# A Fox attention head's division cut into halves of 512 columns between the row maxima, with one row maximum a turn sooner

## The chip, the cores and the metric

The kernel runs on one core of one Trainium2 chip. The metric is the device time of one execution in microseconds; the time of a kernel is the median of its runs.

## What is computed

The reference is one decoder block over 1024 tokens of width 1024. Two branches read one normalised input: a state-space recurrence and an attention with forget gates (Fox). Gates merge them, one projection follows, then attention over 256 memory tokens and a feed-forward layer. The change lies in the Fox attention, 8 heads of 64 columns. Its core in the reference, cut:

```python
s = jnp.einsum('bhqd,bhkd->bhqk', qb, kh).astype(jnp.float32) * scale
s = s + cb[..., :, None] - cum[..., None, :]
s = jnp.where(causal, s, -jnp.inf)
p = jax.nn.softmax(s, axis=-1)
return jnp.einsum('bhqk,bhkd->bhqd', p.astype(vh.dtype), vh)
```

## The kernel before

Every product is made of three matmuls: an operand is split into a high part (a copy on ScalarE) and a low part (the rest, a subtraction on VectorE), and high times high, high times low and low times high are added in one bank (mm3, L173 to L175; split, L183 and L184). PSUM has eight banks: three named mm for projections and row maxima, two named sc for scores, two named pv for values, one named misc.

The Fox attention is one loop over heads (Fox.run), which takes 355 to 571 us of the span. Each head has twelve units (qc, kt): query half qc of 512 columns against key block kt of 128, causal, so units at the diagonal have 512, 384, 256 or 128 columns. A unit is:

- two score matmuls into a sc bank (L1793, L1794), at the diagonal a mask addition on VectorE (L1796), and the exponential on ScalarE (L1800) into pf;
- the split of pf: high part ph on ScalarE (L1805) and low part pl on VectorE (L1806); for the units (0,2), (1,0), (1,2) and (1,4) ph is a cast on VectorE (L1802) and pl a subtraction on GpSimd (L1803);
- one or two units later the products with the values: L1818 and L1819 with ph, L1825 with pl, into a pv bank. At the end of a query half ScalarE copies the bank to num (L1827).

The values carry a column of ones, so row 64 of num is the softmax's denominator. After a head's last unit finish(h) sends it through three small DMAs on SyncE's queue (rc L1836, rd_d L1838, rb L1840) with a reciprocal between them, so that rb holds the reciprocals on 64 partitions. The division divide(h-1) comes in the next head's units: VectorE multiplies num by rb (L1846), ScalarE copies the result to its high part ahi (L183), VectorE subtracts for the low part alo (L184), and both go to DRAM (L1852), or, for the last two heads, straight into the tiles that the output projection reads (L1857).

Into the units of head h other work is woven by tables. PSLOT places the projections of head h+2 (triples L173 to L175 over uh, ul, whi and wlo), which ScalarE and VectorE bring out of PSUM (L1725 to L1733). RSLOT places the row maxima of head h+1: twelve matmuls (L1763) of up to 512 columns, each reduced on VectorE, below the diagonal by L1768 and at the diagonal by L1765. Once all are there, max_row, in unit 9, reduces them to one column per row block (L1776, mboth), TensorE transposes that (L1778), VectorE negates it (L1780), and a DMA writes it to a row of the next head's queries (L1781): the next head's scores subtract the maximum by it. In head loop 6 a second table, RSLOT_LATE, holds the row maxima. Head loop 7 has no further head to prepare; in its place stand matmuls of the GLU stage, whose weights (raw<-wg_d) and the reads of the attention result (att_d into ath and atl, L1882) are also SyncE's DMAs. The split of the weights of head h+3 (whi, wlo) comes in unit 9.

The tables and the code give an order per engine only in part: a scheduler places each instruction by estimated durations, and behind(...) binds an instruction to come after another one in its engine's order. The division stands behind `left`, the last pl subtraction on VectorE. Every engine then works its list strictly in order.

Of the kernel before, what the change touches and what calls it, by code (L numbers as in the profile page):

```python
# [10 lines left out]
F32R = mybir.dt.float32r  # L11
# [26 lines left out]
RSLOT = (1, 2, 2, 3, 4, 4, 5, 6, 7, 7, 8, 8)  # L38
# [1539 lines left out]
class Fox:  # L1578
# [91 lines left out]
    def setup(self):  # L1670
# [16 lines left out]
        self.pj, self.mc, self.pvs, self.num, self.rb, self.raw = {}, {}, {}, {}, {}, {}  # L1687
# [56 lines left out]
    def row_max(self, h):  # L1744
# [11 lines left out]
        def step(qb, b):  # L1756
# [7 lines left out]
            if b == qb // 4:  # L1764
                B.V.tensor_tensor_reduce(out=B.junk[:, :n], in0=ps[:, :n], in1=self.tri[:, 512 - n:512], scale=1.0,  # L1765
                                         scalar=-3.0e38, op0=ALU.add, op1=ALU.max, accum_out=mc[:, 0, qb:qb + 1])
            else:
                B.V.tensor_reduce(out=mc[:, 1, qb:qb + 1], in_=ps, axis=AX.X, op=ALU.max)  # L1768
# [15 lines left out]
    def scores(self, h, qc, kt):  # L1784
# [16 lines left out]
        if (qc, kt) in ((0, 2), (1, 0), (1, 2), (1, 4)):  # L1801
            V.tensor_copy(ph[:, off:], pf[:, off:])  # L1802
            G.tensor_sub(pl[:, off:], pf[:, off:], f32(ph[:, off:]))  # L1803
# [39 lines left out]
    def divide(self, h):  # L1843
        B, S = self.B, self.B.S
        num, rb = self.num.pop(h), self.rb.pop(h)
        B.V.tensor_mul(num[0:64, :], num[0:64, :], rb)  # L1846
        hi = self.fp.tile([64, L], F32R, tag="rb", bufs=2, name="ahi")
        lo = self.fp.tile([64, L], F32R, tag="rb", bufs=2, name="alo")
        B.split(hi, lo, num[0:64, :])
        if h < NH - 2:  # L1850
            for i, a in enumerate((hi, lo)):
                S.dma_start(self.att_d[i, h * DH:(h + 1) * DH, :], f32(a))  # L1852
        else:
            r = slice((h % 2) * DH, (h % 2 + 1) * DH)
            for hf in range(2):
                for dst, a in zip(self.aT.rhs(h // 2, hf), (hi, lo)):
                    S.dma_start(f32(dst[r, :]), f32(a[:, 512 * hf:512 * hf + 512]))  # L1857

    def run(self, y_d, yT, aT, w_glu, w_d, filler):
# [51 lines left out]
        with B.behind(turned):  # L1911
            self.values_of_v(0, 6, ready)
        units = [(qc, kt) for qc in range(2) for kt in range(4 * qc + 4)]
        for h in range(NH):
# [31 lines left out]
            for i, u in enumerate(units):  # L1946
                self.scores(h, *u)
                for f in side[i]:
                    f()
                if len(self.hi_todo) > 2:  # L1950
# [10 lines left out]
        self.divide(NH - 1)  # L1961
# [29 lines left out]
```

## Time and profile before

| | us |
|---|---|
| median of 3 runs | 1540.55 (1540.17 to 1541.73) |
| the profiled execution | 1539.77 |
| its span | 1538.1 |
| TensorE busy | 1520.7 (99%) |
| VectorE busy | 1005.7 (65%) |
| ScalarE busy | 658.1 (43%) |
| GpSimd busy | 253.6 (16%) |

The granted clock was 0.999. The profile shows one execution. Its rows give for each engine a start, a duration, the line and the tiles (out<-in) with their sizes; in brackets stands the time for which the engine had been idle before the instruction, and what ended that. Matmuls overlap, so their cadence is read from start to start. "Head loop h" is the loop's turn h; it divides head h-1 and takes the row maxima of head h+1.

### The profile page before, as it was taken

The page shows a single profiled execution, that of the slowest core. Times are in us where ns is not written, and L with a number is a line of the kernel's source. Part 1 is how long each engine was busy: PE and PEld are TensorE (multiplying, and loading weights), DVE is VectorE, ACT ScalarE, POOL GpSimd, SP SyncE. Part 2 cuts the span into 40 slices and gives each one's busy share as a digit, 9 for nine tenths or more (in the row PEclk, how much of TensorE's full clock was granted, in tenths as well). Part 3 has the DMA queues.
Part 4 walks back from the last instruction along what each step waited for, and adds up shares of the span by engine and source line. Part 5 has one row for each costly group of instructions (what it writes and reads, how often), then busy time and mean ns, then how long its engine had stood idle before and what let it go on. Part 6 is the DMA issues. An engine that isn't in the chain of part 4 may idle for free. (4 is left out here: it accounts for less than half of the span.)

```text
span 1538.1 us, 20434 instructions
## 1 busy us (share of the span) xinstructions
PE 1520.7 (99%) x7329; PEld 1257.7 (82%) x7329; DVE 1005.7 (65%) x1828; ACT 658.1 (43%) x1183; POOL 253.6 (16%) x341
## 2 busy tenths in 40 slices
PE   8999999999999999999999999999999999999998
PEld 7888888898777678888888888888888888888886
DVE  7936554355878867675556797777777775675555
ACT  7423334324667643232435663333333333354343
POOL 1166542100121214100102200000000000101001
PEclk9999999999999999999999999999999999999999
DMA  9634556611223746378210356555544544896542
GB/s 286 161 104 102 131 128 144 180 41 16 50 46 88 192 131 198 111 218 308 89 69 1 117 204 210 162 161 160 158 158 157 157 145 139 291 391 220 192 163 110
DMA packets 196293, 234.06 MB, mean 152 GB/s; under 512 B 35576, under 2 KB 127656, under 8 KB 195680
## 3 DMA queue, kind: packets, MB, share of 16 engines
q1 hardware_dynamic: 188704, 214.93, 47.0%
q10 hardware_dynamic: 7488, 17.83, 3.1%
q8 instruction: 57, 0.93, 0.3%
q14 instruction: 44, 0.36, 0.1%
HBM read 161.94 MB, written 72.71 MB: 153 GB/s over the span
## 5 line engine op out<-in xcount | busy, mean ns | idle before, releaser
L184 DVE TENSOR_TENSOR wlo<-raw,whi 128x1024 fp32r<-128x1024 f32 (+2 forms) x120 | 126.3, 1058 | 45.4 <-ACT whi L183 44.2
L183 ACT CAST whi<-raw 128x1024 fp32r<-128x1024 f32 (+2 forms) x120 | 108.7, 910 | 105.6 <-PE mm L174 39.1
L184 DVE TENSOR_TENSOR ol<-or,oh 128x1024 fp32r<-128x1024 f32 x73 | 90.1, 1236 | 74.0 <-ACT oh L183 71.9
L173 PE MATMUL mm<-uh,whi 128*128 128x512 f32 x344 | 136.5, 397 | 0.0
L174 PE MATMUL mm<-ul,whi 128*128 128x512 f32 x344 | 135.1, 393 | 0.0
L175 PE MATMUL mm<-uh,wlo 128*128 128x512 f32 x344 | 134.5, 391 | 0.0
L183 ACT CAST oh<-or 128x1024 fp32r<-128x1024 f32 x73 | 76.9, 1054 | 105.0 <-PE mm L1108 34.2
L997 POOL TENSOR_TENSOR g<-a,c 128x512 f32<-128x512 f32 x22 | 35.7, 1621 | 389.0 <-ACT a L996 389.0
L175 PEld LDWEIGHTS mm<-uh,wlo 128*128 128x128 f32 x344 | 64.7, 188 | 13.3 <-DVE wlo L184 0.2
L1803 POOL TENSOR_TENSOR pl<-pf,ph 128x512 fp32r<-128x512 f32 (+1 forms) x32 | 36.8, 1152 | 232.5 <-DVE ph L1802 193.3
L173 PEld LDWEIGHTS mm<-uh,whi 128*128 128x128 f32 x344 | 64.8, 188 | 11.6
L174 PEld LDWEIGHTS mm<-ul,whi 128*128 128x128 f32 x344 | 64.8, 188 | 11.0
L1800 ACT ACTIVATE pf<-sc 128x512 f32<-128x512 f32 (+1 forms) x96 | 46.4, 489 | 44.5 <-DVE sc L1796 28.3
L986 DVE SCALAR_TENSOR_TENSOR c<-c,pv 128x512 f32<-128x512 f32 x22 | 15.1, 687 | 76.5 <-ACT c L985 76.4
L211 POOL TENSOR_TENSOR r<-ms,mhalf 128x1 f32<-128x1 f32 (+1 forms) x26 | 15.7, 605 | 298.6 <-DVE ms L207 258.5
L964 PE MATMUL pv<-S3h,we 128*128 128x512 f32 x176 | 57.7, 389 | 0.0
L1806 DVE TENSOR_TENSOR pl<-pf,ph 128x512 fp32r<-128x512 f32 (+2 forms) x64 | 35.3, 553 | 10.4 <-ACT ph L1805 9.8
L1108 PE MATMUL mm<-ol,oh 128*128 128x512 f32 (+1 forms) x110 | 41.9, 381 | 0.0
L1108 PE MATMUL mm<-oh,ol 128*128 128x512 f32 (+1 forms) x110 | 41.9, 381 | 0.0
L1108 PE MATMUL mm<-oh 128*128 128x512 f32 (+1 forms) x110 | 41.9, 381 | 0.0
L173 PE MATMUL sc<-uh,whi 128*128 128x512 f32 x104 | 40.8, 392 | 0.0
L173 PE MATMUL mm<-yh,whi 128*128 128x512 f32 x104 | 40.7, 392 | 0.0
(639 smaller groups left out, 4554.2 us busy)
## 6 DMA issues: line engine op xcount, KB each, us to landing
or<-c_d SPq DMA_DIRECT2D x77, 256.0 KB
wo<-in_w_ffn_out_dram SPq DMA_DIRECT2D x22, 512.0 KB
c_d<-g SPq DMA_DIRECT2D x44, 256.0 KB
t_d<-wo SPq DMA_DIRECT2D x44, 256.0 KB
or<-t_d SPq DMA_DIRECT2D x44, 256.0 KB
rawb<-in_w_ffn_in_dram SPq DMA_DIRECT2D x20, 512.0 KB
raw<-in_w_ffn_in_dram SPq DMA_DIRECT2D x20, 512.0 KB
raw<-in_w_in_dram SPq DMA_DIRECT2D x19, 512.0 KB
```

What stands on the lines that cost most here:

```text
L173: T.matmul(ps, lh, rh, start=first, stop=False)
L174: T.matmul(ps, lh, rl, start=False, stop=False)
L175: return T.matmul(ps, ll, rh, start=False, stop=last)
L183: cast = self.A.copy(hi, src)
L184: self.rest = (self.G if pool_lo else self.V).tensor_sub(lo, src, f32(hi))
L211: self.G.tensor_tensor(out=r, in0=v, in1=self.mhalf[:, 0:n], op=ALU.pow)
L964: T.matmul(ps, l_[:, k, :], r_, start=first and k == 0 and i == 0, stop=k == 3 and i == 2, skip_group_check=True)
L997: G.tensor_mul(g[:, 512:], a1, c1)
L1108: T.matmul(ps, l_[:, gi], r_[:, c0:c1], start=k == 0 and (p == NP - LAST if own else p == 0 and n in (1, 2, 7)), stop=p == NP - 1 and k == ...
L1800: self.exp = A.activation(pf[:, off:], ps[:, off:], AF.Exp)
L1803: G.tensor_sub(pl[:, off:], pf[:, off:], f32(ph[:, off:]))
L1806: self.left = V.tensor_sub(pl[:, off:], pf[:, off:], f32(ph[:, off:]))
```

## The change

The index 8 of RSLOT, the first half of row block 6's maximum (512 columns, L1768), moves from unit 7 to unit 6. The division gets an argument n and is cut into four pieces. Piece 0 multiplies columns 0 to 511; piece 1 multiplies the other half and issues both of ScalarE's copies, each 64x512; pieces 2 and 3 subtract one half each, and the DMAs follow piece 3 (for the last two heads each half's DMAs follow its subtraction). Two new marks are kept: `reduced`, the last row maximum reduced, and `mark`, the last cast of ph on VectorE. From head loop 2 on, piece 0 stands in unit 5 behind `reduced` and `left`, and pieces 1 to 3 in unit 6 behind `reduced` and `mark`; in head loop 1 all four stand in unit 6 behind `reduced` and `mark`. The division after the loop is the four pieces in a row. Line numbers past L1765 are one higher in the new kernel, and more from the division on.

```diff
-RSLOT = (1, 2, 2, 3, 4, 4, 5, 6, 7, 7, 8, 8)
+RSLOT = (1, 2, 2, 3, 4, 4, 5, 6, 6, 7, 8, 8)
...
-                B.V.tensor_reduce(out=mc[:, 1, qb:qb + 1], in_=ps, axis=AX.X, op=ALU.max)
+                self.reduced = B.V.tensor_reduce(out=mc[:, 1, qb:qb + 1], in_=ps, axis=AX.X, op=ALU.max)
...
-            V.tensor_copy(ph[:, off:], pf[:, off:])
+            self.mark = V.tensor_copy(ph[:, off:], pf[:, off:])
...
-    def divide(self, h):
+    def divide(self, h, n):
         B, S = self.B, self.B.S
-        num, rb = self.num.pop(h), self.rb.pop(h)
-        B.V.tensor_mul(num[0:64, :], num[0:64, :], rb)
-        hi = self.fp.tile([64, L], F32R, tag="rb", bufs=2, name="ahi")
-        lo = self.fp.tile([64, L], F32R, tag="rb", bufs=2, name="alo")
-        B.split(hi, lo, num[0:64, :])
-        if h < NH - 2:
+        if n < 2:
+            num, cs = self.num[h], slice(512 * n, 512 * n + 512)
+            B.V.tensor_mul(num[0:64, cs], num[0:64, cs], self.rb[h][:, cs])
+            if n == 0:
+                return
+            self.rb.pop(h)
+            hi, lo = self.quot[h] = [self.fp.tile([64, L], F32R, tag="rb", bufs=2, name=n_) for n_ in ("ahi", "alo")]
+            for hf in range(2):
+                cs = slice(512 * hf, 512 * hf + 512)
+                B.A.copy(hi[:, cs], num[0:64, cs])
+            return
+        hf, num, (hi, lo) = n - 2, self.num[h], self.quot[h]
+        cs = slice(512 * hf, 512 * hf + 512)
+        B.V.tensor_sub(lo[:, cs], num[0:64, cs], f32(hi[:, cs]))
...
+        pieces = {(False, 5): ((0, ("reduced", "left")),),
+                  (False, 6): ((1, ("reduced", "mark")), (2, ("reduced", "mark")), (3, ("reduced", "mark"))),
+                  (True, 6): tuple((n, ("reduced", "mark")) for n in range(4))}
...
+                for n, after in pieces.get((h == 1, i), ()) if h else ():
+                    with B.behind(*(getattr(self, a) for a in after)):
+                        self.divide(h - 1, n)
...
-                if h and i == 5:
-                    with B.behind(self.left):
-                        self.divide(h - 1)
...
-        self.divide(NH - 1)
+        for n in range(4):
+            self.divide(NH - 1, n)
```

How this moves the instructions, at three places. First VectorE in head loop 1, where head 0 is divided; before:

```order
L1802 CAST ph<-pf 128x512
L1846 TENSOR_TENSOR num<-num,rb 64x1024
L1768 TENSOR_REDUCE mc<-mm 128x1
L1727 SCALAR_TENSOR_TENSOR hb_3274<-mm,hb_3273 64x512
L184 TENSOR_TENSOR alo<-num,ahi 64x1024
L1806 TENSOR_TENSOR pl<-pf,ph 128x512
L1765 ISA junk,mc<-mm,tri 128x384
L1765 ISA mc 128x1
```

And after, the same place:

```order
L1803 CAST ph<-pf 128x512
L1769 TENSOR_REDUCE mc<-mm 128x1
L1848 TENSOR_TENSOR num<-num,rb 64x512 x2
L1765 ISA junk,mc<-mm,tri 128x384
L1765 ISA mc 128x1
L1859 TENSOR_TENSOR alo<-num,ahi 64x512
L1727 SCALAR_TENSOR_TENSOR hb_3274<-mm,hb_3273 64x512
L1859 TENSOR_TENSOR alo<-num,ahi 64x512
L1807 TENSOR_TENSOR pl<-pf,ph 128x512
```

Both multiplications now stand behind the first half of row block 6's maximum, and its second half (384 columns) ahead of the subtractions. Next VectorE some steps on in head loop 1, where the maxima are brought together; before:

```order
L1806 TENSOR_TENSOR pl<-pf,ph 128x384
L1765 ISA junk,mc<-mm,tri 128x512
L1765 ISA mc 128x1
L1776 TENSOR_REDUCE mboth<-mc 128x8
L1759 MEMSET mc 128x8
L184 TENSOR_TENSOR wlo<-raw,whi 128x1024
```

And after:

```order
L1765 ISA junk,mc<-mm,tri 128x512
L1765 ISA mc 128x1
L184 TENSOR_TENSOR wlo<-raw,whi 128x1024
L1807 TENSOR_TENSOR pl<-pf,ph 128x384
L1777 TENSOR_REDUCE mboth<-mc 128x8
L1797 TENSOR_TENSOR sc<-sc,trk 128x128 x2
```

The weight subtraction (wlo) stood behind mboth and now stands ahead of it; in head loops 2 to 4 it stays behind. Last TensorE at the end of head loop 2, where the next head's first scores begin (the first two scores are the pairs with 512 and 384 columns; uh and ul are the projections' operands); before:

```order
L1825 MATMUL pv<-pl,vhi 65x256
L173 MATMUL mm<-uh_0_89,whi 128x512
L174 MATMUL mm<-ul_0_97,whi 128x512
L175 MATMUL mm<-uh_0_89,wlo 128x512
L1793 MATMUL sc<-hb_3273,hb_3271 128x512
L1794 MATMUL sc<-hb_3274,hb_3272 128x512
L1793 MATMUL sc<-hb_3273,hb_3271 128x384
L1794 MATMUL sc<-hb_3274,hb_3272 128x384
L1825 MATMUL pv<-pl,vhi 65x128
```

And after:

```order
L175 MATMUL mm<-uh_0_87,wlo 128x512
L1794 MATMUL sc<-hb_3273,hb_3271 128x512
L1795 MATMUL sc<-hb_3274,hb_3272 128x512
L173 MATMUL mm<-uh_0_87,whi 128x512
L174 MATMUL mm<-ul_0_95,whi 128x512
L175 MATMUL mm<-uh_0_87,wlo 128x512
L1819 MATMUL pv<-ph,vhi 65x256
L1820 MATMUL pv<-ph,vlo 64x256
L1826 MATMUL pv<-pl,vhi 65x384
L1794 MATMUL sc<-hb_3273,hb_3271 128x384
L1795 MATMUL sc<-hb_3274,hb_3272 128x384
```

The first score stands fifteen matmuls sooner, the second a little less. The transposition of the maxima stands seven rows sooner in head loops 2 to 4, right behind the second matmul of a projection triple, and three matmuls later in head loop 1. In head loop 2 VectorE's list from the division to mboth now reads: first half of the multiplication, ph, the maximum's first half, second half of the multiplication, its 384-column half, both subtractions, pl, a mask addition, the next maximum, an evacuation (L1727), ph, the last maximum, a mask addition, mboth.

Elsewhere: in head loop 6 both subtractions now stand ahead of two mask additions that stood ahead of the subtraction. In SyncE's list seven reads of att_d now stand ahead of the weights of the GLU's fourth column block (two DMAs), which ScalarE now splits in head loop 7, between the exponentials of the units (0,2) and (0,3), instead of in head loop 6; the second of the two loads stands behind the rc DMA of head 6. GpSimd's list is the same.

More of the change, by code (lines that the diff above doesn't have):

```diff
@@ L1686, in setup @@
         self.maxed = self.scored = None
-        self.pj, self.mc, self.pvs, self.num, self.rb, self.raw = {}, {}, {}, {}, {}, {}
+        self.pj, self.mc, self.pvs, self.num, self.rb, self.raw, self.quot = {}, {}, {}, {}, {}, {}, {}
         self.hi_todo, self.lo_todo, self.spread, self.maxima = [], [], {}, {}
```

15 lines of the change are left out of this document (8 added, 7 removed).

## The prediction

> **What bounds the kernel now.** I read the profile's page first, then the table of stretches over the attention, then what TensorE waited for there, and last the timelines of single engines around the waits. The page:
>
> ```profile
> span 1538.1 us, 20434 instructions
> PE 1520.7 (99%) x7329; PEld 1257.7 (82%) x7329; DVE 1005.7 (65%) x1828; ACT 658.1 (43%) x1183; POOL 253.6 (16%) x341
> ```
>
> TensorE is busy for 99% of the span, so an edit that neither adds nor removes a matmul can only win what TensorE waits, or make it wait. The stretches, one row each (from:to, length, then busy time of TensorE, its weight loads, VectorE, ScalarE and GpSimd): head loop 2, most of head loop 5, and the 49 us behind the head loops.
>
> ```profile
> 424.60:449.40 24.80, 24.77 (x124) 18.88 (x123) 20.26 (x51) 16.75 (x32) 4.61 (x4) 1.00 0.30 55
> 499.00:519.00 20.00, 19.04 (x92) 13.40 (x91) 18.43 (x50) 13.87 (x28) 4.61 (x4) 1.00 0.69 168
> 571.00:620.00 49.00, 49.00 (x219) 40.56 (x218) 35.18 (x35) 16.65 (x23) 16.73 (x10) 1.00 0.56 166
> ```
>
> VectorE, the engine the change loads, has 4.5 us idle per head in head loop 2 (24.80 less 20.26), and 1.6 in the head loop 5 stretch. The two largest rows of TensorE's waits between 355 and 590 us (total, times, longest):
>
> ```profile
> PE mm L1763 <- DVE mc L1768: 1.2, 1, 1.2
> PE sc L1793 <- ACT pf L1800: 0.7, 2, 0.5
> ```
>
> The first is the one wait that the change plainly addresses: a row-maximum matmul that waits for a bank which VectorE has not yet reduced. It lies in head loop 1. VectorE there:
>
> ```profile
> 407.85 0.43 DVE L1802 CAST ph<-pf 128x512 fp32r<-128x512 f32 x1
> 408.69 2.04 DVE L1846 TENSOR_TENSOR num<-num,rb 64x1024 f32<-64x1024 f32 x1 [0.41 <-DMA rb<-rd_d]
> 410.65 0.67 DVE L1768 TENSOR_REDUCE mc<-mm 128x1 f32<-128x512 f32 x1
> ...
> 418.32 0.17 DVE L1776 TENSOR_REDUCE mboth<-mc 128x8 f32<-128x16 f32 x1
> ...
> 418.63 1.22 DVE L184 TENSOR_TENSOR wlo<-raw,whi 128x1024 fp32r<-128x1024 f32 x1
> ```
>
> TensorE and GpSimd beside it:
>
> ```profile
> 409.74 0.40 PE L1818 MATMUL pv<-ph,vhi 128*65 128x512 f32 x1
> 411.38 0.44 PE L1763 MATMUL mm<-hb 68*128 68x384 f32 x1 [1.24 <-DVE mc L1768]
> ...
> 418.62 0.27 PE L1778 MATMUL misc<-ident,mboth 128*8 128x128 f32 x1
> ```
>
> ```profile
> 408.36 1.29 POOL L1803 TENSOR_TENSOR pl<-pf,ph 128x512 fp32r<-128x512 f32 x1 [2.80 <-DVE ph L1802]
> ```
>
> The reader is to see the order: the whole multiplication stood ahead of the reduction, began inside GpSimd's subtraction and lasted 2.04 us; the reduction came at 410.65, the matmul at 411.38.
>
> **The change part by part.** The sum is made against the profiled execution (span 1538.1 us, 1539.77 in all), which stands 0.78 under the median 1540.55; I add the difference to the median.
>
> *Head loop 1: the wait goes, the next one is the maxima's transposition.* Now the reduction stands right behind the probability cast: it can begin at 408.28 (407.85 + 0.43) instead of 410.65, and the 384-column matmul finds its bank free. That returns 1.24. What is late next is L1776, on which the transposition L1778 waits. Before, 7.67 us lay between the reduction and L1776 (410.65 to 418.32). Into this stretch come the multiplication (1.21) and the weight subtraction (1.22), which the new order puts ahead of L1776, and some 0.2 for the halves; one mask addition and the waits of the old queue leave it, about 0.6 to 0.9 together (my estimate). So L1776 begins at 408.28 + 7.67 + 2.63 less 0.6 to 0.9, which is 417.7 to 418.0, and up to 0.7 later where the first half still meets GpSimd's subtraction (408.36 to 409.65). TensorE would reach the transposition, moved behind three more matmuls (0.35), at 418.62 - 1.24 + 0.35 = 417.73. With the 0.17 of L1776 it waits 0.15 to 1.1 there; I take 0.5. Net -0.75, bounds 0 and -1.24.
>
> *Head loops 2 to 4: earlier scores against an earlier transposition.* At the start of head loop 3 TensorE shows this:
>
> ```profile
> 449.82 0.23 PE L1763 MATMUL mm<-hb 68*128 68x128 f32 x1
> 450.08 0.39 PE L1793 MATMUL sc<-hb,hb 69*128 69x256 f32 x1
> 450.30 0.29 PE L1794 MATMUL sc<-hb,hb 128*128 128x256 f32 x1
> 450.43 0.28 PE L1763 MATMUL mm<-hb 68*128 68x256 f32 x1
> ```
>
> 256 columns take 0.13 (450.30 to 450.43), yet the 128-column matmul holds 0.26 and the next 0.22: about 0.3 us lost, because the third score of the new head wants the bank of the first, which the exponential is still reading (the second wait row above). In the new order the first two scores of heads 3 and 4 stand fifteen and fourteen matmuls sooner, of head 2 two, the exponential is done earlier, and the loss can go: at most 0.9 over the three boundaries of this kind.
>
> But the transposition also stands seven rows sooner, and its chain on VectorE is not shorter. Head loop 2 now, VectorE, then TensorE:
>
> ```profile
> 433.78 1.21 DVE L1846 TENSOR_TENSOR num<-num,rb 64x1024 f32<-64x1024 f32 x1
> 434.92 0.41 DVE L1802 CAST ph<-pf 128x512 fp32r<-128x512 f32 x1
> ...
> 442.36 0.68 DVE L1765 CUSTOM_DVE_ANT_0 junk<-mm,tri 128x512 bf16<-128x512 f32 x1
> 442.97 0.07 DVE L1765 DVE_READ_ACCUMULATOR2_ANT mc<- 128x1 f32 x1
> ```
>
> ```profile
> 441.19 0.40 PE L174 MATMUL mm<-ul,whi 128*128 128x512 f32 x1
> 441.43 0.49 PE L1763 MATMUL mm<-hb,hb 68*128 68x512 f32 x1
> ```
>
> A 512-column step lets the next begin 0.61 later (442.36 to 442.97). After the first half (433.78 + 0.61) and the cast (0.37) the queue holds, up to L1776, ten steps of 0.36 to 0.65 and two mask additions of 0.2: about 6.2 us, to 441.0. The second half begins inside GpSimd's subtraction, which starts with the end of the cast and lasts 1.29; a multiplication that began so took 2.04 instead of 1.21 (head loop 1), so I add 0.8: 441.8, with L1776 itself 442.0. TensorE reaches the transposition at 441.43 + 0.23 (one more row-maximum matmul ahead) = 441.66. So it waits 0.3 in each of three heads, and wins 0.3 at each boundary: net 0, bounds -0.9 (no wait) and +1.5 (0.8 each for the wait, boundaries as hoped). The DMA of the maxima's row follows the transposition on SyncE; no score waited for it before, so no row shows what margin it has before the earlier scores, and C holds that too.
>
> The Trainium skill ("SBUF — State Buffer", section "Who interferes with whom") gives the reason: a VectorE instruction with two SBUF inputs and a GpSimd instruction that reads SBUF exclude each other for the whole of the one that started first. The 2.04 beside the 1.29 agrees. The rule speaks against this place for the second half: by it the three transpositions wait as above, and without it the sum would be 0.9 lower.
>
> *What halving costs.* From the forms of the attention (mean ns of one) and the division's own line:
>
> ```profile
> L1729 DVE TENSOR_TENSOR hb<-mm,hb 64x512 fp32r<-64x512 f32 x10 | 6.9, 694 | 0.3
> L1726 ACT CAST hb<-mm 64x512 fp32r<-64x512 f32 x10 | 5.8, 583 | 3.9 <-PE sc L1793 3.8
> L183 ACT CAST ahi<-num 64x1024 fp32r<-64x1024 f32 x7 | 7.3, 1047 | 6.4 <-DVE num L1846 6.4
> ```
>
> ```profile
> L1846 DVE TENSOR_TENSOR num<-num,rb x8: 1208/1214/2039, 408.7 to 581.1; 64x1024 f32<-64x1024 f32 x8
> ```
>
> On VectorE two pairs at 2 x 0.69 instead of 1.21 are 0.35 more a head, on ScalarE 2 x 0.58 instead of 1.05 are 0.12. The idle 4.5 us hide it in head loops 2 to 4; what reaches L1776 is in the chains above. In head loop 5 the 1.6 us of idle are thin: the maximum now stands ahead of the multiplication, the halves lengthen the rest; 0, bounds -0.5 and +0.5. The last division lies in a stretch where TensorE never idled (49.00 of 49.00): 0.
>
> *Head loop 6: mask additions behind both subtractions.*
>
> ```profile
> 535.07 1.22 DVE L1846 TENSOR_TENSOR num<-num,rb 64x1024 f32<-64x1024 f32 x1 [0.45 <-DMA rb<-rd_d]
> ...
> 536.82 0.48 DVE L1796 TENSOR_TENSOR sc<-sc,trk 128x128 f32<-128x128 f32 x2
> 537.40 1.22 DVE L184 TENSOR_TENSOR alo<-num,ahi 64x1024 fp32r<-64x1024 f32 x1
> ```
>
> The two additions stood ahead of the subtraction and now stand behind its halves, 1.2 us later; the two exponentials and so the score banks follow. Five more matmuls (1.1 us) now stand ahead of the next score in TensorE's order and hide most of it; the multiplication's halves and ScalarE's add 0.3. I take +0.4, bounds 0 and +0.9.
>
> *Sum:* -0.75 + 0 + 0 + 0.4 = -0.35; median 1540.2. With all bounds it reaches from -2.6 to +2.9.
>
> **The rivals.**
>
> *A, everything opens.* VectorE's queue has more slack than I counted, no transposition waits, the mask additions are hidden: -1.24 - 0.9 = -2.1, with head loop 5's -0.5 up to -2.6: 1538.4, at best 1537.9. For it: 4.5 us of idle per head. Against it: the chains above end at or behind TensorE's arrival. 0.17.
>
> *B, GLU weights come late.* In SyncE's queue the seven reads of the attention result now stand ahead of the fourth block of GLU weights, whose second load falls behind rc of head 6. SyncE, ScalarE and TensorE around it:
>
> ```profile
> 527.76 0.43 SPq L158 DMA_DIRECT2D raw<-wg_d  x1
> ...
> 529.31 0.46 SPq L1840 DMA_DIRECT2D rb<-rd_d  x1
> ...
> 543.99 0.53 SPq L1836 DMA_DIRECT2D rc<-num  x1
> ```
>
> ```profile
> 530.67 1.05 ACT L183 CAST whi<-raw 128x1024 fp32r<-128x1024 f32 x1 [0.44 <-DMA raw<-wg_d]
> ...
> 547.02 0.38 ACT L1800 ACTIVATE pf<-sc 128x256 f32<-128x256 f32 x1
> ```
>
> ```profile
> 549.61 0.40 PE L1793 MATMUL sc<-hb,hb 69*128 69x512 f32 x1
> ```
>
> The load would be issued at 543.99 + 0.53 = 544.5. A weight load took 2.9 us to the cast (527.76 to 530.67), rb 5.8 us to its reader (529.31 to 535.07): it lands between 547.4 and 550.3. The cast now stands on ScalarE behind the 256-column exponential (547.40) and ahead of the next one, whose bank the score at 549.61 needs; with 1.05 and about 0.3 for both, a landing after 548.3 costs what it is late, up to 2.0: 1540.2 to 1542.2. 0.13.
>
> *C, the maxima's row becomes the limit (the slower side).* Place: L1778 in head loops 1 to 5. My chains hold no wait inside VectorE's queue except GpSimd's; every subtraction that waits for ScalarE's half, or a second meeting with GpSimd, goes straight to the transposition, since TensorE already arrives 0.3 before it. It decides from there: 1.0 us more in each of five heads is +5.0, so +4.6 in all, 1545.2; 0.5 each gives 1542.7. For it: the chain to L1776 holds 1.6 us more in head loop 1, and in each head two conversions that wait for ScalarE. Against it: ScalarE is 67% busy in head loop 2 (16.75 of 24.80), the first conversion only needs the first half. 0.12.
>
> *D, nothing moves.* The order does change, but in head loop 1 the transposition takes back all of the 1.24 and the rest cancels: 1540.5 to 1540.9. 0.13.
>
> My forecast keeps 0.45.
>
> **How the numbers follow.** About 0.2%, 3.1 us, is what a measurement of this kernel can tell from no change: faster means below 1537.5, slower above 1543.6. Below lie only the ends of A and the best of the forecast's bounds: 0.05. Above lies the heavier half of C, and its meeting with B: 0.07. The rest, 0.88, is the same. The range goes from 1538.0 (A, nearly whole) to 1542.7 (C at half a microsecond each, or B whole with head loop 6's upper bound).
>
> **What would show it.** In the changed profile the row of L1763 waiting for L1768 is gone; the transposition (one line later) shows waits for the maxima's row of a few tenths in head loops 1 to 4; the multiplication's halves last 0.69, and one of two in head loops 2 to 4 about 1.4; the waits of the first scores' bank shrink. I am wrong if VectorE's second halves show no lengthening, if the transposition waits over a microsecond, if the fourth GLU cast lands after 548.3, or if TensorE's busy time itself changes.

## The result, and the profile after

| us | before | after |
|---|---|---|
| median (lowest to highest of 5 runs each) | 1540.55 (1540.12 to 1541.73) | 1546.39 (1545.66 to 1548.39) |
| the profiled execution | 1539.77 | 1545.66 |
| its span | 1538.1 | 1543.3 |

The changed kernel is slower by 5.84 us: ratio 1.0038, interval 1.0025 to 1.0051. That lies outside the range of the prediction, on the side of its rival C. The page of the changed kernel, the same two lines as before:

```profile
span 1543.3 us, 20474 instructions
PE 1522.9 (99%) x7329; PEld 1257.6 (81%) x7329; DVE 1009.6 (65%) x1844; ACT 658.8 (43%) x1191; POOL 258.4 (17%) x341
```

VectorE's busy time grew by 3.9 us in a span that grew by 5.2; the number of matmuls is the same. So the question is where TensorE waits. Its waits between 355 and 600 us (total, times, longest):

```profile
PE mm L1763 <- ACT hb L1733: 2.1, 2, 1.2
PE sc L1794 <- ACT pf L1801: 1.8, 3, 1.3
PE misc L1779 <- DVE mboth L1777: 0.6, 2, 0.4
```

The row that led the list before (L1763 behind the reduction L1768, 1.2) is gone, as predicted. Two rows that were 0.3 and 0.7 are now 2.1 and 1.8: a bank of a projection, which ScalarE empties at L1733, and a score bank, which the exponential reads.

To place the loss I counted the matmuls. Both kernels issue 7329. The starts of the matmuls 1940, 2110, 2275, 2400, 2520, 2640, 2755, 2830 and 2960 (361.7, 391.7, 426.9, 452.3, 476.9, 502.0, 526.3, 543.5 and 570.9 us before) cut the attention into the loops; the table gives how much longer the changed kernel took for each piece, up to the last matmul.

| ahead | loop 0 | 1 | 2 | 3 | 4 | 5 | 6 | 7 | behind | all |
|---|---|---|---|---|---|---|---|---|---|---|
| +0.60 | +0.01 | -0.98 | +2.06 | +1.56 | +1.13 | -0.23 | +0.97 | 0.00 | -0.08 | +5.05 |

The 0.60 arise ahead of anything that changed; single executions differ by as much. The cuts count matmuls, and their order differs a little: at the ends of loops 1 and 4 the changed kernel has issued 384 columns fewer, which is 0.17 us (512 columns take 0.23). So loop 1 won about 0.8, loop 2 lost about 1.9 and loop 4 about 1.3; the sum of loops 2 to 4 stays 4.75, nearly all of the 5.05.

**Head loop 1.** VectorE, then TensorE, in the changed kernel:

```profile
408.79 0.69 DVE L1769 TENSOR_REDUCE mc<-mm 128x1 f32<-128x512 f32 x1
409.39 1.87 DVE L1848 TENSOR_TENSOR num<-num,rb 64x512 f32<-64x512 f32 x2
...
418.69 0.16 DVE L1777 TENSOR_REDUCE mboth<-mc 128x8 f32<-128x16 f32 x1
```

```profile
409.63 0.34 PE L1763 MATMUL mm<-hb 68*128 68x384 f32 x1
...
418.91 0.27 PE L1779 MATMUL misc<-ident,mboth 128*8 128x128 f32 x1 [0.21 <-DVE mboth L1777]
```

The 384-column matmul has no bracket: the wait of 1.24 is gone, and the transposition takes back 0.21. This is the part of the change that does what it says.

**Head loop 2, the loss from its start.** VectorE first, then ScalarE, from 439 us on:

```profile
438.95 0.28 DVE L1797 TENSOR_TENSOR sc<-sc,trk 128x128 f32<-128x128 f32 x1
439.15 0.67 DVE L1769 TENSOR_REDUCE mc<-mm 128x1 f32<-128x512 f32 x1
...
440.91 0.68 DVE L1765 CUSTOM_DVE_ANT_0 junk<-mm,tri 128x512 bf16<-128x512 f32 x1
441.52 0.08 DVE L1765 DVE_READ_ACCUMULATOR2_ANT mc<- 128x1 f32 x1
441.52 0.29 DVE L1797 TENSOR_TENSOR sc<-sc,trk 128x128 f32<-128x128 f32 x1
441.72 0.16 DVE L1777 TENSOR_REDUCE mboth<-mc 128x8 f32<-128x16 f32 x1
```

```profile
439.32 0.60 ACT L1801 ACTIVATE pf<-sc 128x512 f32<-128x512 f32 x1 [0.29 <-DVE sc L1797]
441.93 0.49 ACT L1801 ACTIVATE pf<-sc 128x384 f32<-128x384 f32 x1 [2.01 <-DVE mboth L1777]
...
443.67 0.59 ACT L1732 ACTIVATE hb<-mm 64x512 fp32r<-64x512 f32 x1
...
448.78 0.59 ACT L1732 ACTIVATE hb<-mm 64x512 fp32r<-64x512 f32 x1 [1.56 <-DVE hb L1729]
449.38 0.58 ACT L1733 CAST hb<-mm 64x512 fp32r<-64x512 f32 x1
449.99 0.60 ACT L1801 ACTIVATE pf<-sc 128x512 f32<-128x512 f32 x1
```

The same places in the kernel before:

```profile
439.05 0.54 DVE L1796 TENSOR_TENSOR sc<-sc,trk 128x128 f32<-128x128 f32 x2
```

```profile
439.43 0.98 ACT L1800 ACTIVATE pf<-sc 128x512 f32<-128x512 f32 x2 [0.76 <-DVE sc L1796]
440.35 0.59 ACT L1732 ACTIVATE hb<-mm 64x512 fp32r<-64x512 f32 x1
...
448.21 0.58 ACT L1733 CAST hb<-mm 64x512 fp32r<-64x512 f32 x1
449.43 0.60 ACT L1800 ACTIVATE pf<-sc 128x512 f32<-128x512 f32 x1 [0.64 <-DVE sc L1796]
```

Before, the mask additions of the units (1,4) and (1,5) stood together (x2, from 439.05), and the two exponentials ran together. Now the addition of (1,5) stands behind both halves of row block 7's maximum, at 441.52. ScalarE can't begin that exponential, nor, since it works its list in order, anything behind it: it idles 2.01 us. (The profile names mboth as the releaser; the exponential reads only what the mask addition wrote, which ended 0.07 earlier.) The evacuation that stood at 440.35 now stands at 443.67. From 441.93 to 447.2 ScalarE works without a pause, but doesn't catch up: VectorE's L1729 waits for it, ScalarE's next L1732 for that, and L1733 ends at 449.96 instead of 448.79. TensorE behind it:

```profile
448.85 0.22 PE L1763 MATMUL mm<-hb 68*128 68x128 f32 x1
450.01 0.38 PE L1763 MATMUL mm<-hb 68*128 68x256 f32 x1 [0.94 <-ACT hb L1733]
450.63 0.39 PE L1794 MATMUL sc<-hb,hb 69*128 69x256 f32 x1 [0.24 <-ACT pf L1801]
```

TensorE's list has moved as well. The new head's first score ran at 446.00, 2.4 us sooner than before (448.43), its second nine matmuls sooner, its third five, and the 128-column maximum, at 448.85 instead of 449.82, six. Just ahead of the first score, where both kernels have issued the same matmuls, the changed one was 0.32 behind (445.77 against 445.45), so that most of what loop 1 had won was already spent. Then it waits for the bank of L1733, and once more for the first score's: ScalarE came to that exponential at 449.99 instead of 449.43. At the next place with the same matmuls issued TensorE was 1.70 behind (453.81 against 452.10). The next boundary loses it in one piece:

```profile
477.02 0.39 PE L1794 MATMUL sc<-hb 69*128 69x256 f32 x1 [1.34 <-ACT pf L1801]
```

### The profile page after: what moved, and what is told of

Its sections match the earlier page's. It is cut to its first block, busy times and chain, and to the rows that moved or that the text cites. A ratio compares the mean times of both kernels' runs of the same rounds, so it can differ in the third digit from the quotient of the medians.

```text
span 1543.3 us, 20474 instructions
## 1 busy us (share of the span) xinstructions
PE 1522.9 (99%) x7329; PEld 1257.6 (81%) x7329; DVE 1009.6 (65%) x1844; ACT 658.8 (43%) x1191; POOL 258.4 (17%) x341
## 5 line engine op out<-in xcount | busy, mean ns | idle before, releaser
L1252 POOL TENSOR_TENSOR sg<-sg,ga 128x512 f32<-128x512 f32 x16 | 30.1, 1902 | 72.1 <-DVE sg L1245 70.7
```

The lines of the kernel that those rows point to most:

```text
L1252: self.B.G.tensor_mul(self.out[j][:, cs], self.out[j][:, cs], ga)
```

## The experiments

Two theories: *order*, that the mask addition of (1,5) behind row block 7's maxima delays ScalarE and so the banks at the boundary (the end of a loop, where the next head's first scores stand); and *load*, that the halves themselves (more work on VectorE, and second meetings with GpSimd) cost the time. A third question came up on the way: what happens in loops 5 and 6. Beside these twelve kernels the kernel before had medians of 1540.07 to 1540.48. The table gives the median, the ratio with its interval, and, from the one profiled execution each, how much longer each head loop took than before; an execution's own offset ahead of the attention (0.1 to 1.6) is left out. The cuts shift some of it here too: at the end of loop 1 by 0.17, as in the changed kernel, in all but e3, g2, g4, g8 and e5; at the end of loop 4 by 0.17 in all but e4 and g8, in f1 the other way; and loop 6 stands 0.3 too high in e3 and g6 and 0.5 in g4.

| kernel | median | ratio (interval) | loop 1 | 2 | 3 | 4 | 5 | 6 |
|---|---|---|---|---|---|---|---|---|
| e1_max_sooner | 1542.82 | 1.0016 (1.0007 to 1.0025) | -0.29 | +1.95 | +0.31 | +1.09 | -0.77 | +0.33 |
| e3_halves_unit5 | 1546.42 | 1.0038 (1.0026 to 1.0051) | -0.01 | +1.45 | +1.04 | +1.18 | +0.10 | +1.77 |
| e4_head1_only | 1540.11 | 0.9998 (0.9990 to 1.0007) | -0.81 | +0.40 | 0.00 | +0.18 | +0.01 | -0.54 |
| f1_rb7_unit9 | 1545.85 | 1.0037 (1.0023 to 1.0050) | -0.46 | +0.90 | +0.50 | +1.51 | +1.22 | +1.58 |
| g1_ahead | 1545.14 | 1.0033 (1.0020 to 1.0045) | -0.95 | +0.73 | +0.32 | +0.78 | +1.23 | +2.38 |
| g2_mask_behind | 1542.36 | 1.0013 (1.0004 to 1.0021) | -1.30 | +1.13 | +1.10 | +0.47 | -0.79 | +0.70 |
| g4_halves_ahead | 1546.12 | 1.0038 (1.0025 to 1.0050) | -0.15 | +0.28 | +0.29 | +0.89 | +1.38 | +4.58 |
| g6_loops1to4_ahead | 1544.12 | 1.0026 (1.0015 to 1.0036) | -0.82 | +0.75 | +0.31 | +1.22 | -0.21 | +1.97 |
| g7_ahead_2_3 | 1543.65 | 1.0022 (1.0012 to 1.0033) | -0.99 | +0.77 | +0.31 | +1.47 | -0.10 | +1.50 |
| g8_head1_whole | 1539.78 | 0.9996 (0.9987 to 1.0005) | -0.79 | +0.04 | 0.00 | +0.17 | +0.02 | -0.34 |
| g5_loops1to4 | 1544.95 | 1.0035 (1.0022 to 1.0048) | -0.84 | +2.08 | +1.58 | +1.12 | -0.76 | +0.63 |
| e5_whole_new_place | 1543.13 | 1.0018 (1.0009 to 1.0027) | -0.97 | +0.56 | +0.48 | +0.78 | -0.46 | +0.86 |

### Each part alone

**e1_max_sooner**: the kernel before with the new table; the division stays whole, in unit 5 behind `left`.

```diff
-RSLOT = (1, 2, 2, 3, 4, 4, 5, 6, 7, 7, 8, 8)
+RSLOT = (1, 2, 2, 3, 4, 4, 5, 6, 6, 7, 8, 8)
```

> The kernel before with the table's one entry changed (row block 6's first maximum in unit 6) and the division as it was, whole and in unit 5. Two theories. Order: the loss comes from where the mask addition of unit (1,5) lands in VectorE's list; behind the last row maxima it holds up that unit's exponential, with it ScalarE's evacuations of the projections and the next head's first exponential, and TensorE then waits at the start of the next head for a mm or sc bank. In this kernel the mask addition lands there too, in head loops 2 to 5, so order expects most of the loss without any halving: 1542.5 to 1546. Load: the loss is what the halves cost VectorE (twice two starts more a head, and the second multiplication held by GpSimd); this kernel has no halves, so load expects 1539.5 to 1541.

Measured 1542.82. No division is halved here, and the boundary of loop 2 is lost all the same: ScalarE idles the same 2.01 us for the same mask addition.

```profile
442.61 0.49 ACT L1800 ACTIVATE pf<-sc 128x384 f32<-128x384 f32 x1 [2.01 <-DVE mboth L1776]
```

TensorE's third score, which needs the bank of the first, waits 1.27 there. And loop 1 keeps a wait of 1.1 for L1768: with the multiplication still ahead of the reduction, the sooner maximum alone doesn't free the bank. So a loss of this kind needs no halves, and the sooner maximum alone, with the division whole, costs 2.5 us.

**e3_halves_unit5**: the changed kernel with the old table, all four pieces in unit 5 behind `left`.

```diff
-RSLOT = (1, 2, 2, 3, 4, 4, 5, 6, 6, 7, 8, 8)
+RSLOT = (1, 2, 2, 3, 4, 4, 5, 6, 7, 7, 8, 8)
...
+        pieces = {(False, 5): tuple((n, ("left",)) for n in range(4)),
+                  (True, 5): tuple((n, ("left",)) for n in range(4))}
```

> The kernel before with the division in four pieces that all stand in unit 5 behind the last pl subtraction, and the old table. The mask addition lands behind the last row maxima in head loops 2 and 4 only, while head loops 3 and 5 keep their boundary. Order expects about half of the loss, at the boundaries behind head loops 2 and 4 alone: 1542 to 1544.5. Load expects all of the loss, since every head has its halves: 1545.5 to 1547.

Measured 1546.42: as slow as the whole change and inside the range of *load*, where *order* as I had put it asked for half of that. The trace says where the time goes. In loops 2 and 4 the mask addition of (1,5) stands behind row block 7's maxima here too (ScalarE idles 2.00 in loop 2). In loops 1 and 3 a reduction stands behind both multiplications, and TensorE waits 1.3 and 1.1 for it. In both places the halves met a GpSimd subtraction and took 1.77 and 2.38 together, where two undisturbed ones take 1.28. So the halves do cost here: by their place in the list, and by the meetings with GpSimd that *load* names.

**e4_head1_only** and **g8_head1_whole**: the new table and the new place of the division in head loop 1 alone, all else as before; in e4 four pieces, in g8 the whole division in one.

```diff
+RSLOT_1 = (1, 2, 2, 3, 4, 4, 5, 6, 6, 7, 8, 8)
...
-                    side[(RSLOT_LATE if late else RSLOT)[i]].append(f)
+                    side[(RSLOT_LATE if late else RSLOT_1 if h == 1 else RSLOT)[i]].append(f)
```

> The change in head loop 1 alone: there the sooner maximum and the division in four pieces behind it, in all other head loops and after the loop the kernel before. Order expects the 1.24 wait of head loop 1 gone with some 0.5 given back at the transposition, and unchanged boundaries behind head loops 2 to 5: 1539.3 to 1540.5. Load expects one head's share of the loss less the gain: 1540.5 to 1541.5.

> The sooner maximum in head loop 1 alone, with the division there whole and behind it, and the kernel before in all else. Both theories: the wait of head loop 1 for its row maximum goes without any halving, and the transposition gives less back than with halves, since the weight subtraction stays behind mboth: head loop 1 gains 0.7 to 1.2, 1539.2 to 1540.3. If halving were needed to win the wait: 1540.3 to 1541.

Measured 1540.11 and 1539.78. Loop 1 wins 0.81 and 0.79 (e4 about 0.64 without the cut's shift), nearly as much as in the changed kernel, so the gain is a matter of the order in which multiplication and reduction stand, not of halving. g8, VectorE:

```profile
408.43 0.69 DVE L1770 TENSOR_REDUCE mc<-mm 128x1 f32<-128x512 f32 x1
409.04 1.80 DVE L1848 TENSOR_TENSOR num<-num,rb 64x1024 f32<-64x1024 f32 x1
```

The whole multiplication takes 1.80 here, the two halves of the changed kernel 1.87 together. Over loops 1 and 2 e4 is 0.34 behind g8. Not all of that is shown to be the halving: around the end of loop 1, from the matmul 2263 to the matmul 2283, where all issue the same matmuls in slightly different orders, e4 took 4.09, but e1, which halves nothing, took 4.10 as well (g8 3.95, the kernel before 3.90). Neither kernel is clearly faster than before: a gain of 0.8 us is 0.05%, and the intervals hold 1.

### The mask addition by itself

**g2_mask_behind**: the kernel before, with nothing of the change, but for one edge: in loops 2 to 4 the mask addition of (1,5) must stand behind the last maximum of row block 7 (`reduced`).

```diff
-            V.tensor_add(ps[:, off:off + P], ps[:, off:off + P], self.trk)
+            with B.behind(self.reduced if 1 < h < 5 and (qc, kt) == (1, 5) else None):
+                V.tensor_add(ps[:, off:off + P], ps[:, off:off + P], self.trk)
```

> The kernel before with one edge more: in head loops 2 to 4 the mask addition of unit (1,5) has to stand behind the last maximum of row block 7 on VectorE. Table and division are as before. Order expects the boundaries' waits from this edge alone, about 1.0 to 1.5 behind each of the three head loops: 1543 to 1545.5. Load expects nothing but the addition's own shift: 1540 to 1541.2.

Measured 1542.36: slower than before, by less than *order* asked for and more than *load*. The place is the same. ScalarE, then TensorE:

```profile
441.91 0.49 ACT L1801 ACTIVATE pf<-sc 128x384 f32<-128x384 f32 x1 [1.10 <-DVE mboth L1776]
...
447.67 0.58 ACT L1733 CAST hb<-mm 64x512 fp32r<-64x512 f32 x1
448.28 0.60 ACT L1801 ACTIVATE pf<-sc 128x512 f32<-128x512 f32 x1
```

```profile
448.93 0.39 PE L1793 MATMUL sc<-hb,hb 69*128 69x256 f32 x1 [0.68 <-ACT pf L1801]
```

ScalarE idles 1.10 instead of 2.01 because the scheduler put both evacuations (L1732, L1733) ahead of the late exponential, and TensorE loses 0.8 to 1.0 at each of the three boundaries instead of 1.3 to 1.6. Loops 2 to 4 lose 2.70, without any of the change's other parts. So this one edge, with the lists that the scheduler makes of it, is enough for a loss of this kind. But the loss doesn't come by way of ScalarE here. Just ahead of the boundary of loop 2, g2 was 0.45 ahead of the kernel before, so undelayed it would reach L1733 at 447.76 and the first exponential at 448.98; it reached them at 447.67 and 448.28. ScalarE had made up its idle time. What had moved is TensorE's list: with the edge the scheduler put the new head's first score twelve matmuls sooner and the third seven, more than the exponential had gained.

**g7_ahead_2_3**: the reverse. The changed kernel, but in loops 2 and 3 the scores of (1,5) are issued one unit sooner, so that the scheduler puts its mask addition ahead of the maxima again. The lists of loops 1, 5, 6 and 7 stay as in the changed kernel.

```diff
-                self.scores(h, *u)
+                if not (h in (2, 3) and i == 9):
+                    self.scores(h, *u)
+                if h in (2, 3) and i == 8:
+                    self.scores(h, *units[9])
```

> The changed kernel with the scores of unit (1,5) one unit sooner in head loops 2 and 3 only. The lists of all engines in head loops 1, 5, 6 and 7 read as in the changed kernel, so nothing else moves in this one. Order: TensorE's time from the start to the end of head loops 2 and 3 falls from 2.06 and 1.56 over the kernel before to about 0.7 and 0.3 (what the earlier run with head loops 2 to 5 showed there), the rest stays: 1543.3 to 1544.6. Load, the halves' own cost, stays in every head: 1545.7 to 1547.

Measured 1543.65, inside what *order* gave. Loops 2 and 3 lose 1.08 where the changed kernel lost 3.62; loop 4, left alone, still loses its boundary (1.1 for L1733). VectorE, ScalarE and TensorE in loop 2:

```profile
439.19 0.48 DVE L1797 TENSOR_TENSOR sc<-sc,trk 128x128 f32<-128x128 f32 x2
```

```profile
439.56 0.98 ACT L1801 ACTIVATE pf<-sc 128x512 f32<-128x512 f32 x2 [0.29 <-DVE sc L1797]
...
449.43 0.58 ACT L1733 CAST hb<-mm 64x512 fp32r<-64x512 f32 x1
450.04 0.60 ACT L1801 ACTIVATE pf<-sc 128x512 f32<-128x512 f32 x1
```

```profile
448.93 0.40 PE L1794 MATMUL sc<-hb,hb 69*128 69x512 f32 x1
...
450.32 0.23 PE L1763 MATMUL mm<-hb 68*128 68x128 f32 x1
450.69 0.38 PE L1794 MATMUL sc<-hb,hb 69*128 69x256 f32 x1
```

The two additions and the two exponentials are together again. One thing here corrects the plain form of the theory: ScalarE reaches L1733 and the first exponential at 449.43 and 450.04, no sooner than in the changed kernel (449.38 and 449.99). What else differs is TensorE's list: the new head's first score stands at 448.93, where it stood before the change, and the matmul that wants L1733's bank and the third score come later in the list, with other work ahead of them. In the changed kernel the scheduler had moved TensorE's matmuls forward, and ScalarE's work had not come forward with them. The loss is the gap between the two.

The other kernels agree. Counted with the changed kernel, the table gives 39 boundaries at the ends of loops 2 to 4. In 14 of them the addition of (1,5) stands behind the last maximum; in all of these the next head's first score stands eleven to fifteen matmuls sooner, and TensorE loses 0.3 to 1.4 us between places up to which it has issued the same matmuls as before. In the other 25 the first score stands where it stood or one matmul sooner, and TensorE loses 0.2 at most. So the late addition and the moved scores always come together, and g2 and g7 are what tells them apart: in g2 ScalarE came in time and the loss was there, in g7 ScalarE came at the same times as in the changed kernel and the loss was down to 0.1. The moved scores are the larger part. An estimate for loop 2 of the changed kernel says the same: with TensorE's old list its third score would have come at 450.08 + 0.32 = 450.40, and the exponential ahead of it ended at 450.59, so ScalarE's lateness alone would have cost about 0.2 of the 1.38. No run keeps TensorE's list and delays the addition, so the split stays an estimate.

### The same cure in more loops, and what it ran into

**g1_ahead** does g7's edit in loops 2 to 5 of the changed kernel; **g4_halves_ahead** does it in loops 2 to 5 of e3.

```diff
-                self.scores(h, *u)
+                if not (h in (2, 3, 4, 5) and i == 9):
+                    self.scores(h, *u)
+                if h in (2, 3, 4, 5) and i == 8:
+                    self.scores(h, *units[9])
```

> The changed kernel with the scores of unit (1,5) issued one unit sooner in head loops 2 to 5, so that their mask addition stands ahead of row block 7's maxima in VectorE's list, as in the kernel before; table, halves and marks stay. The first four runs changed the two theories. Order now says: the late mask addition costs the 1.3 to 1.5 us at each boundary behind head loops 2 to 4, and another order costs more in head loops 5 to 7 by chance of the cascade (the maxima there stand behind a multiplication that waits for rb, as when the maxima of row block 7 were moved to unit 9, about 3.5). It expects no wait over 0.6 at the three boundaries, about 3.5 less there than the change, and 1542 to 1545 in all. Load, the halves' own cost in every head, expects the time of the change: 1545.5 to 1547.

> The division in four pieces in unit 5 with the old table (1546.4 before), and the scores of unit (1,5) one unit sooner in head loops 2 to 5. Order expects the boundaries behind head loops 2 and 4 to lose their waits (1.5 and 1.25), the maxima that stand behind the multiplication in head loops 1 and 3 (1.5 and 1.26) and in head loop 6 to keep theirs: 1543 to 1545. Load expects no change: 1545.8 to 1547.

Measured 1545.14 and 1546.12. Loops 2 to 4 fall from 4.75 to 1.83 and from 3.67 to 1.46, but the medians hardly move, since loops 5 and 6 take it back (+3.61 in g1 against +0.74 in the changed kernel; loop 6 of g4 alone +4.58, with a wait of 1.6 for a GpSimd subtraction, in an execution that was the slowest of its five and 1.8 above their median). So the totals missed what *order* gave, and g4's lies in the range of *load*, while the loops that the cure addressed did what *order* says.

**f1_rb7_unit9** puts row block 7's maxima a unit later instead.

```diff
-RSLOT = (1, 2, 2, 3, 4, 4, 5, 6, 6, 7, 8, 8)
+RSLOT = (1, 2, 2, 3, 4, 4, 5, 6, 6, 7, 9, 9)
```

> The changed kernel with the two maxima of row block 7 entered in unit 9 instead of unit 8, so that the mask addition of unit (1,5) stands ahead of both in VectorE's list; halves, marks and the sooner maximum stay. Order expects the boundary waits to go: 1539.5 to 1542. Load expects no change, since VectorE does the same work beside the same GpSimd: 1545.5 to 1547.

Measured 1545.85, a miss of *order* and inside the range of *load*. The waits at the boundaries fell to 0.2, none and 0.4, but the later maxima brought four waits of up to 0.4 of their own, and loops 5 and 6 lost 2.80. In loop 6 of f1, VectorE and TensorE:

```profile
539.25 1.28 DVE L1848 TENSOR_TENSOR num<-num,rb 64x512 f32<-64x512 f32 x2 [1.78 <-DMA rb<-rd_d]
...
542.27 0.67 DVE L1769 TENSOR_REDUCE mc<-mm 128x1 f32<-128x512 f32 x1
```

```profile
543.00 0.50 PE L173 MATMUL mm<-yh,whi 128*128 128x512 f32 x1 [1.60 <-DVE mc L1769]
```

The multiplication waits for its reciprocals from DRAM, and a maximum that stands behind it waits too, with the bank that TensorE wants. In the changed kernel that maximum stood ahead of the multiplication, at 538.31. The same pattern stands in e3 and g1 (idle times of 2.02 and 2.46 for rb). In f1 the reciprocals come no later than in the changed kernel (the multiplication begins at 539.25 and 539.84): what changed is that less stands ahead of the multiplication in VectorE's list.

**g5_loops1to4** confines the change to loops 1 to 4 (whole division and old table from loop 5 on), and **g6_loops1to4_ahead** adds g7's edit in loops 2 to 4.

```diff
-                    side[(RSLOT_LATE if late else RSLOT)[i]].append(f)
+                    side[(RSLOT_LATE if late else RSLOT_1 if 0 < h < 5 else RSLOT)[i]].append(f)
```

> The change in head loops 1 to 4, the whole division in unit 5 and the old table in head loop 5 and after. Head loops 1 to 4 read as in the changed kernel. Order: their steps (-1.0, +2.1, +1.6, +1.1) stay, and head loop 6, whose two mask additions stand ahead of the subtraction again, loses less than the 0.97 of the change: 1544.7 to 1546.2. Load expects half of the loss to be left, three of six heads being whole: 1543 to 1544.

> The sooner maximum and the four pieces in head loops 1 to 4 only, the whole division in head loops 5 to 7 and after them, and the scores of unit (1,5) one unit sooner in head loops 2 to 4. Order expects the 1.24 of head loop 1 partly won, no boundary waits over 0.6, and what is left to come from head loop 6, where the multiplication stands ahead of a maximum and waits for rb (0.5 to 2): 1540 to 1542.5. Load expects four of six heads' share of the loss: 1543.5 to 1545.

Measured 1544.95 and 1544.12. g5 repeats the changed kernel's loops 1 to 4 to a tenth (4.78 against 4.75 in loops 2 to 4), so that loss needs nothing of what changed in loops 5 and 6. g6 missed what *order* asked for: loops 2 and 3 were cured (+1.06), loop 4 still lost 1.22, only 0.2 of it at its boundary, for a reason that isn't shown, and loop 6 lost 1.97. *Load* had named a range that holds the total, but its place, the halves in loops 2 to 4, doesn't show it.

**e5_whole_new_place**: the changed kernel with the division whole, in unit 6 behind `reduced` and `mark` in every loop.

```diff
+        pieces = {(False, 6): ((0, ("reduced", "mark")),), (True, 6): ((0, ("reduced", "mark")),)}
...
-                        self.divide(h - 1, n)
+                        self.divide_whole(h - 1)
```

> The sooner maximum and the new place of the division (unit 6, behind the reduction and the cast) in all head loops, but the division whole. In head loops 2 to 5 the mask addition of unit (1,5) stands one maximum later than in the kernel before, yet ahead of the last one, and TensorE's list at the head boundaries is that of the kernel before. Order expects boundaries without long waits: head loop 1 gains 0.8, head loops 2 to 4 lose 0 to 0.5 each, head loop 6 loses up to 1: 1539.7 to 1542. If the place behind the reduction were what costs, without the halves, it would come near the change: 1544 to 1546.5.

Measured 1543.13, about 1 above *order*'s range and 1 below the other. With one piece instead of four the scheduler keeps the mask addition of (1,5) ahead of the last maximum, and no boundary has a long wait:

```profile
439.96 0.28 DVE L1797 TENSOR_TENSOR sc<-sc,trk 128x128 f32<-128x128 f32 x1
...
440.63 0.69 DVE L1765 CUSTOM_DVE_ANT_0 junk<-mm,tri 128x512 bf16<-128x512 f32 x1
```

```profile
449.29 0.60 ACT L1801 ACTIVATE pf<-sc 128x512 f32<-128x512 f32 x1
```

The first exponential of head 3 starts at 449.29, and TensorE, whose list there is that of the kernel before, was 0.15 ahead of it; so ScalarE stands to TensorE as it did (449.43). What is left, 0.56, 0.48 and 0.78 in loops 2 to 4 and 0.86 in loop 6, shows in part as waits of 0.2 for a maximum and one of 0.6 for the transposition in loop 6. It is a price of the new place without the late addition.

By the medians alone neither theory wins: *order*'s range held in e1, e4, g5 and g7, *load*'s in e3, f1, g4 and g6, both in g8, and neither in g1, g2 and e5. The account below rests on the places in the traces at which TensorE waits.

## Why the prediction was wrong, step by step

**Head loop 1** was right: -0.98 in the profiled execution, or about -0.8 without the cut's shift, where I took -0.75 with bounds of 0 and -1.24; e4 and g8 measured -0.81 and -0.79 for it alone. L1777 came at 418.69, and at 418.1 without the 0.60 that arose ahead of the attention, inside what I had worked out (417.7 to 418.0, up to 0.7 later).

**Head loops 2 to 4** are where it failed: net 0 with bounds -0.9 and +1.5, and +4.75 came. The failed step is this sentence of it: "In the new order the first two scores of heads 3 and 4 stand fifteen and fourteen matmuls sooner, of head 2 two, the exponential is done earlier, and the loss can go". The scores did come sooner (446.00 instead of 448.43), and head 5's as well, which the sentence leaves out. The exponential did not (449.99 instead of 449.43): it is ScalarE's, and ScalarE's list was held up 2.01 us by a mask addition. And the matmuls that need the banks came sooner too: the third score, which needs the first one's, five matmuls, the 256-column maximum, which needs that of L1733, eight. So TensorE stood there and waited.

I had followed VectorE's list to mboth, since the transposition hangs on that, and the mask addition stands in my own list of it, behind the last maximum; I priced it as 0.2 us of VectorE's time and didn't ask who waits for it.

The boundaries, at which I expected to win 0.3 each, lost 1.61, 1.50 and 1.33, worked out as the cadence of the matmuls there less that of undisturbed ones; that is 1.38, 1.38 and 0.92 more than the kernel before lost there, 3.7 of the 4.75. g2 shows that the late addition, with the lists that come of it, makes such a loss, g7 that undoing it takes the loss at the boundary down to 0.1, and ScalarE's times in both that the matmuls moved forward weigh more than ScalarE's idle time.

The other half of this term, the transposition, I had priced too high: I expected waits of 0.3 in three heads, and the two waits of the changed kernel (0.6 together) are the 0.21 of loop 1 and this one of loop 6:

```profile
543.47 0.27 PE L1779 MATMUL misc<-ident,mboth 128*8 128x128 f32 x1 [0.42 <-DVE mboth L1777]
```

The lengthening that I built them on did come. VectorE and GpSimd in loop 2:

```profile
433.81 0.68 DVE L1848 TENSOR_TENSOR num<-num,rb 64x512 f32<-64x512 f32 x1
...
435.35 1.39 DVE L1848 TENSOR_TENSOR num<-num,rb 64x512 f32<-64x512 f32 x1
```

```profile
434.90 1.29 POOL L1804 TENSOR_TENSOR pl<-pf,ph 128x512 fp32r<-128x512 f32 x1 [3.17 <-DVE ph L1803]
```

The second half began 0.45 inside GpSimd's subtraction and took 0.71 more than the first. That agrees with the Trainium skill ("SBUF — State Buffer", section "Who interferes with whom"), by which the two exclude each other for the whole of the one that began first. The rule held; it wasn't what set the time.

**Halving** at 0 was nearly right: 0.34 at most over loops 1 and 2, in e4 against g8. Two halves in a row cost VectorE less than I had added, 1.28 for a pair of subtractions against 1.22 for the whole. **Head loop 5**, 0 within 0.5, came at -0.23 (-0.4 without the cut's shift). **Head loop 6**, +0.4 with a bound of 0.9, came at +0.97, the direction right and the size just over the bound, but the mechanism isn't shown: in the second half of the loop TensorE waits 0.42 for the transposition and 0.2 for a ph, not for a score bank, and g5, in which the two mask additions stand ahead of the subtraction again, lost 0.63 there too. **The last division** cost nothing, as said.

**Rival B** didn't decide. The second weight load stands behind rc, as feared, and ScalarE's cast waits for it:

```profile
549.11 0.53 SPq L1837 DMA_DIRECT2D rc<-num  x1
550.02 0.36 SPq L158 DMA_DIRECT2D raw<-wg_d  x1
```

```profile
552.95 1.05 ACT L183 CAST whi<-raw 128x1024 fp32r<-128x1024 f32 x1 [0.88 <-DMA raw<-wg_d]
```

It came 2.9 us after its issue, the short end of my bounds. With the 5.1 us that the kernel was behind by then, that is 547.8 of before, ahead of the 548.3 from which I had it cost; loop 7 took as long as before. **Rival C** had the sign and nearly the size, but not the place: it put the loss at the transposition, which hardly waited.

**What stays open.** How the loss at the boundaries divides between TensorE's moved list and ScalarE's lateness is an estimate for one of them. Loops 2 to 4 keep 0.3 to 0.8 each with the mask addition early (g1, g7, e5). In loop 6 alone the twelve kernels differ by 5.1 us (-0.54 to +4.58; about 4.7 without the cut's shift in g4); the one pattern that I can show is the maximum behind a multiplication that waits for rb, and I haven't separated it from what the scheduler moved along with it. And the loop table is of single executions: e5's gave +1.80 in all where its median is 3.06 above that of the kernel before.

## What to carry to other kernels

When an edit reorders an in-order engine's list, follow every instruction that moved back to the one that waits for it on another engine, not only the ones on the chain you have in mind: a 0.3 us mask addition, moved 2.2 us back, held ScalarE for 2 us, and with the lists that the scheduler made around it TensorE lost 0.9 to 1.4 us at three places. A matmul that is moved forward wins nothing until the engine that empties its bank moves forward with it. And where a scheduler makes the lists, cutting one operation into four changes the places of its neighbours on every engine: compare the lists at the loop's ends too, not only around the edit.

## What the hardware showed besides

The wait of 1.24 in head loop 1, at which the change aimed, looks like the outcome of a close race. In g2, whose list there is that of the kernel before, VectorE and GpSimd did this:

```profile
409.02 1.21 DVE L1847 TENSOR_TENSOR num<-num,rb 64x1024 f32<-64x1024 f32 x1
```

```profile
409.19 2.20 POOL L1804 TENSOR_TENSOR pl<-pf,ph 128x512 fp32r<-128x512 f32 x1 [2.81 <-DVE ph L1803]
```

The reciprocals were there when the cast ended, so that the multiplication began first: it took its plain 1.21, GpSimd took 2.20 instead of 1.29, and TensorE's wait for the bank didn't arise (loop 1: -1.30, with none of the change's parts). In the kernel before rb came 0.41 late, GpSimd began first, and the multiplication took 2.04. In these two executions 0.41 us in a DMA's landing went with a wait of 1.24 or none; how often each happens no run shows.
